# 72 of 80 TensorE transposes done as 32x32 blocks on VectorE, with the blocks moved through a DRAM scratch

## The chip, the cores and the metric

The kernel runs on one core of a Trainium2 chip. A core has TensorE (PE in the profile: matmuls, with the weight loads as PEld), VectorE (DVE), ScalarE (ACT), GpSimd (POOL) and SyncE (SP), each with its own instruction queue worked off in order. Transfers are issued from the queues of SP, ACT or POOL. The metric is the device time of one execution in microseconds; of several runs the median is given.

## What is computed

A decoder trunk of two layers over 256 positions of width 2048, all in 32-bit floats. The even layer runs two token mixers beside each other (HGRN2, a gated linear recurrence done in chunks, and RG-LRU, a per-channel recurrence) on one input projection; the odd layer is an mLSTM. Each branch has a gate path. After the output projection and the residual sum comes a gated per-layer embedding. Cut to what the change touches:

```python
h = x
for i in range(2):
    hn = rmsnorm(h, norm[i])
    u = hn @ w_in[i]
    ...                                            # the mixers of the layer
    y = head_rmsnorm(mixed, g) * gate(u)           # g: a_norm (even, HGRN2 half), c_norm (odd)
    h = h + y @ w_out[i]
    pl = rmsnorm(p[i] @ ple_w[i], ple_norm[i])
    h = h + sigmoid(h @ ple_gate_w[i]) * pl
return rmsnorm(h, final_norm)
```

## The kernel before

A tile has 128 partitions. An activation lies either feature-major (features on the partitions, 256 positions along the row) or token-major (128 positions on the partitions, features along the row, two halves `hf`). A matmul contracts over partitions, so what goes into a projection must be feature-major.

Every projection is done with three matmuls, since a float is split into a high part and a rest: ScalarE casts the raw weight to `whi` (L129), VectorE subtracts to get `wlo` (L130), and activations are split the same way into `hi` and `lo` of one tile `ahl`. `load_weights` loads two raw tiles of 128x1024 (512 KB each, SP's queue, L124). There are five raw buffers and four each of `whi` and `wlo`, so ScalarE can cast as soon as TensorE has freed a buffer. `block` is one feature-major block of 128 outputs: 16 matmuls of 512 columns (L160) with both halves of the activation, then 16 of 256 columns (L166). `project_tok` is the token-major form, a pair of 128x512 outputs in four quarters `kq` of 24 matmuls (L201 to L203).

The work beside the projections is written as generators. `start(lane, gen)` puts one into a lane, `pump()`, called once in every block and quarter, advances each lane by one step, and `drain` finishes a lane. A scheduler then sets the order of each queue from priorities: the two split instructions of a weight tile are given a priority 400 places ahead.

Transposes stand in two places. `feature_major` (L458 to L476) takes a finished token-major tile `u` of 2 x 512 features, transposes its eight 128x128 squares on TensorE into two PSUM banks `mx` (L469), and then scales each by the norm's gain and splits it (`scaled_split`: L278 on ScalarE, L279 on VectorE) into the `ahl` tiles `y` that the output projection reads. It is started twice in the even layer (by `combine`, in the stretch of the `ez` projection and the gates behind it) and four times in the odd layer (one for each `oz` projection `j`). `turn` (L1084 to L1091) transposes a quarter `hq[q]` of the residual stream from feature-major to token-major (L1089), four times in the last stage; the `gated` function there reads the result from PSUM as its last addend (L1097). All six and four calls take eight transposes each, 80 in all.

The last stage is three `project_tok` of `g1`, then `quarter(0)` and `quarter(1)`, two projections of half the width (L1129 to L1131) that share the last turn; then come the final norm and the stores.

## Time and profile before

| | |
|---|---|
| median of 3 runs | 1069.3 us (1068.81 to 1069.33) |
| span of the profiled execution, first to last instruction | 1067.3 us |
| TensorE busy | 1053.7 us, 99% |
| VectorE busy | 744.7 us, 70% |
| ScalarE busy | 583.4 us, 55% |
| GpSimd busy | 121.8 us, 11% |
| HBM traffic | 199.25 MB read, 2.10 MB written |

The page gives no time for the profiled execution but its span; the median of the runs lies 2.0 us above it. In the views, a line such as "L130 DVE TENSOR_TENSOR wlo<-raw,whi ... x359 | 455.8, 1294 | 229.4" names source line, engine, operation, output and inputs, and the count; then come busy microseconds in all, mean nanoseconds of one, and the idle time of the engine before it. The chain is followed back from the last instruction; a piece gives its start, its length and what ran. Overlapping matmuls each show their full duration, but on the chain only what each adds.

### The profile page before, as it was taken

How to read it: one execution, taken by the hardware profiler on the slowest of the kernel's cores; microseconds unless marked ns; L12 is line 12 of the kernel's file. 1: busy time of each engine (PE TensorE's matmuls, PEld its weight loads, DVE VectorE, ACT ScalarE, POOL GpSimd, SP SyncE). 2: the span in 40 equal slices, each digit the busy share in tenths (PEclk: the TensorE clock that was granted, in tenths of full speed). 3: DMA queues.
4: the chain of work that ended last, by engine and by line, in shares of the span. 5: the costliest groups of instructions: out<-in, count | busy, mean ns of one | idle time of the engine just before them, and what ended most of it. 6: DMA issues, size and time to landing. Idle time of an engine off the chain costs nothing.

```text
span 1067.3 us, 16069 instructions
## 1 busy us (share of the span) xinstructions
PE 1053.7 (99%) x6128; PEld 906.2 (85%) x6128; DVE 744.7 (70%) x1090; ACT 583.4 (55%) x854; POOL 121.8 (11%) x96
## 2 busy tenths in 40 slices
PE   8999999999999999999999999999999999999996
PEld 7888888888888888888888888888888888888886
DVE  6778997997767557777444877765556577755665
ACT  7665545869554445656444666644445465434543
POOL 0044532511000000112000000000000003000111
PEclk9999999999999999999999999999999999999998
DMA  9755554545746555555555544455555765655552
GB/s 354 287 182 188 198 165 152 178 159 195 239 159 207 188 196 190 187 181 193 191 196 174 180 158 157 145 183 192 195 186 201 237 213 170 198 197 177 178 178 80
DMA packets 57102, 202.39 MB, mean 190 GB/s; under 512 B 6337, under 2 KB 7617, under 8 KB 57025
## 3 DMA queue, kind: packets, MB, share of 16 engines
q1 hardware_dynamic: 55440, 196.65, 54.9%
q0 software_dynamic: 1152, 4.19, 1.2%
q8 instruction: 48, 0.79, 0.3%
q10 hardware_dynamic: 432, 0.52, 0.1%
q14 instruction: 30, 0.24, 0.1%
HBM read 199.25 MB, written 2.10 MB: 189 GB/s over the span
## 4 chain that ended last, share of the span: by engine, by line
PE 99%; ACT 0%; DMA 0%; DVE 0%; ACTq 0%; issue 0%
PE mm L160 33%; PE mm L166 17%; PE mm L201 13%; PE mm L203 13%; PE mm L202 13%; PE mm L1131 1%; PE mm L1129 1%; PE mm L1130 1%; PE mx L750 1%; PE nu L967 1%; PE mx L469 0%; PE mm L149 0%; PE mx L588 0%; PE mm L150 0%; PE mm L151 0%; PE mm L1046 0%
## 5 line engine op out<-in xcount | busy, mean ns | idle before, releaser
L130 DVE TENSOR_TENSOR wlo<-raw,whi 128x1024 fp32r<-128x1024 f32 (+1 forms) x363 | 457.2, 1285 | 229.4 <-ACT whi L129 135.1
L129 ACT CAST whi<-raw 128x1024 fp32r<-128x1024 f32 (+1 forms) x363 | 377.5, 1044 | 329.2 <-PE mm L160 155.0
L160 PE MATMUL mm<-ahl,whi 128*128 128x512 f32 x1536 | 367.3, 391 | 0.0
L160 PEld LDWEIGHTS mm<-ahl,whi 128*128 128x128 f32 x1536 | 282.1, 188 | 56.4 <-DVE ahl L279 0.7
L201 PE MATMUL mm<-whi,ahl 128*128 128x512 f32 x608 | 239.1, 393 | 0.0
L203 PE MATMUL mm<-whi,ahl 128*128 128x512 f32 x608 | 236.8, 390 | 0.0
L202 PE MATMUL mm<-wlo,ahl 128*128 128x512 f32 x608 | 236.7, 389 | 0.0
L166 PE MATMUL mm<-ahl,wlo 128*128 128x256 f32 x1536 | 202.1, 284 | 0.0
L166 PEld LDWEIGHTS mm<-ahl,wlo 128*128 128x128 f32 x1536 | 195.5, 191 | 7.1 <-issue 0.4
L203 PEld LDWEIGHTS mm<-whi,ahl 128*128 128x128 f32 x608 | 114.1, 188 | 24.0
L201 PEld LDWEIGHTS mm<-whi,ahl 128*128 128x128 f32 x608 | 114.2, 188 | 23.2
L202 PEld LDWEIGHTS mm<-wlo,ahl 128*128 128x128 f32 x608 | 114.2, 188 | 23.1
L172 ACT COPY sm<-mm 128x256 f32<-128x256 f32 x64 | 23.6, 368 | 42.5 <-PE mm L166 42.5
L1029 POOL DMA_DIRECT2D row<-in_rows_dram x4 | 2.2, 540 | 356.8 <-DVE u L1019 336.7
L274 POOL TENSOR_TENSOR acc<-acc,sq 128x512 f32<-128x512 f32 x6 | 9.8, 1633 | 193.7 <-ACT sq L273 193.7
L173 DVE TENSOR_TENSOR mg<-mm,sm 128x256 f32<-128x256 f32 x64 | 26.5, 415 | 0.1
L856 DVE SCALAR_TENSOR_TENSOR qk<-mg,prm,qk 128x255 f32<-128x255 f32 (+2 forms) x48 | 21.1, 478 | 5.0 <-ACT qk L853 4.7
L1117 POOL TENSOR_TENSOR pl<-pl,row 128x512 f32<-128x512 f32 x6 | 9.2, 1535 | 124.7 <-ACT sq L1101 124.7
L1129 PE MATMUL mm<-whi,ahl 128*128 128x256 f32 x64 | 18.3, 285 | 0.0
L274 POOL TENSOR_TENSOR placc<-placc,sq 128x512 f32<-128x512 f32 x7 | 11.2, 1607 | 60.2 <-ACT sq L273 59.8
L1130 PE MATMUL mm<-wlo,ahl 128*128 128x256 f32 x64 | 18.1, 283 | 0.0
L1131 PE MATMUL mm<-whi,ahl 128*128 128x256 f32 x64 | 18.1, 283 | 0.0
(294 smaller groups left out, 809.8 us busy)
## 6 DMA issues: line engine op xcount, KB each, us to landing
raw<-in_ew_dram SPq DMA_DIRECT2D x64, 512.0 KB, 4.3
raw<-in_g_dram SPq DMA_DIRECT2D x56, 512.0 KB, 3.9
raw<-in_eo_dram SPq DMA_DIRECT2D x32, 512.0 KB, 4.1
raw<-in_ov_dram SPq DMA_DIRECT2D x32, 512.0 KB, 3.7
raw<-in_oqk_dram SPq DMA_DIRECT2D x32, 512.0 KB, 4.3
raw<-in_oog_dram SPq DMA_DIRECT2D x32, 512.0 KB, 3.9
raw<-in_oz_dram SPq DMA_DIRECT2D x32, 512.0 KB, 3.9
raw<-in_oo_dram SPq DMA_DIRECT2D x32, 512.0 KB, 4.0
```

The lines of the kernel that those rows point to most:

```text
L129: last["act"] = s.copy(h, r).ins
L130: last["dve"] = v.tensor_tensor(out=l, in0=r, in1=h.bitcast(F32), op=ALU.subtract).ins
L160: last["pe"] = te.matmul(ps, parts[k // 8][0][:, c:c + P], act[k // 2][2][:, (k % 2) * 512:(k % 2 + 1) * 512], start=(k == 0), stop=False).ins
L166: last["pe"] = te.matmul(ps[:, T:2 * T], parts[k // 8][1][:, c:c + P], act[k // 2][0][:, k % 2], start=False, stop=(k == KT - 1)).ins
L172: s.copy(small, ps[:, T:2 * T])
L173: v.tensor_tensor(out=dst, in0=ps[:, 0:T], in1=small, op=ALU.add)
L201: te.matmul(ps[hf], xh, wh, start=(k == 0), stop=False)
L202: te.matmul(ps[hf], xh, wl, start=False, stop=False)
L203: last["pe"] = te.matmul(ps[hf], xl, wh, start=False, stop=(k == KT - 1)).ins
L1129: te.matmul(ps[hf], xh, wh, start=(k == 0), stop=False)
L1130: te.matmul(ps[hf], xh, wl, start=False, stop=False)
L1131: last["pe"] = te.matmul(ps[hf], xl, wh, start=False, stop=(k == KT - 1)).ins
```

## The change

`feature_major` and `turn` no longer use TensorE. VectorE's `transpose` turns each 32x32 block where it lies, written to a tile `w` in an order that groups the blocks by their target. A new function `across` writes `w` to a DRAM scratch tile of its own (512 KB) and reads it back with four transfers into `r`, each filling 32 partitions from runs of 1 KB, so that each block gets to its place. All five transfers are issued from ScalarE's queue. In `feature_major` ScalarE then scales from `r` into `xr` and splits that (`split_act`, L144 and L145); in `turn` it copies `r` to a tile `x`, which `gated` reads in place of the PSUM bank. The last of the four calls in the odd layer (j = 3) keeps the old function, under the name `feature_major_pe`; its eight transposes stay on TensorE. The tiles come from buffers of other tiles: in the even layer from the tags `q` and `f`, in the odd layer from a tag `wt` of four 128x1024 buffers, in which `wt` and `scw` of the mixer now lie too. The last turn is started ahead of the third `g1` projection instead of behind it, in the same lane.

```diff
+    def across(w, r, name):
+
+        d = dr.tile([P, 1024], F32, name=name)
+        s.dma_start(out=d, in_=w)
+        yield
+        to = r.rearrange("p (i n) -> p i n", i=4)
+        for j in range(4):
+            s.dma_start(out=to[32 * j:32 * j + 32], in_=d.rearrange("(i q) (j n) -> j q i n", i=4, j=4)[j])
+        yield
+
+    def feature_major(u, gain, first, y, room):
+
+        w = room("w")
+        w5 = w.rearrange("p (j c h t) -> p h c j t", j=4, c=4, h=2)
+        for hf in range(2):
+            v.transpose(w5[:, hf], u[:, hf].rearrange("p (c j q) -> p c j q", c=4, j=4))
+        yield
+        r = room("r")
+        yield from across(w, r, f"du{gain}{first}")
+        r5 = r.rearrange("p (i c h t) -> p c h i t", i=4, c=4, h=2)
+        for b in range(2):
+            x = tp.tile([P, 512], F32, name="xr", tag="hn", bufs=3)
+            for k in range(2):
+                s.activation(x[:, k * T:(k + 1) * T].rearrange("p (h i t) -> p h i t", h=2, i=4), r5[:, 2 * b + k],
+                             AF.Copy, scale=pc(gain, first + 2 * b + k))
+            y[first // 2 + b] = split_act(x, "y")
+
-    def feature_major(u, gain, first, y):
+    def feature_major_pe(u, gain, first, y):
...
-            start("fm", feature_major(u, "cn", 4 * j, y))
+            start("fm", feature_major(u, "cn", 4 * j, y, room) if j < 3 else feature_major_pe(u, "cn", 4 * j, y))
...
         def turn(q, banks):
 
+            w = room("w")
+            w5 = w.rearrange("p (j h c x) -> p h c j x", j=4, h=2, c=4)
             for hf in range(2):
-                ps = px.tile([P, 512], F32, name="mx", tag="mx")
-                for i in range(4):
-                    te.transpose(ps[:, i * P:(i + 1) * P], hq[q][:, i * T + hf * P:i * T + (hf + 1) * P], ident)
-                banks.append(ps)
-                yield
+                v.transpose(w5[:, hf], hq[q].rearrange("p (c h j t) -> p h c j t", c=4, h=2, j=4)[:, hf])
+            yield
+            r = room("r")
+            yield from across(w, r, f"dh{q}")
+            r5 = r.rearrange("p (i h c x) -> p h c i x", i=4, h=2, c=4)
+            x = room("x")
+            for hf in range(2):
+                s.copy(x[:, hf * 512:(hf + 1) * 512].rearrange("p (c i x) -> p c i x", c=4, i=4), r5[:, hf])
+                banks.append(x[:, hf * 512:(hf + 1) * 512])
...
+        banks = [[] for _ in range(4)]
         for g in range(3):
-            banks = []
-            start("tr", turn(g, banks))
+            start("tr", turn(g, banks[g]))
+            if g == 2:
+                start("tr", turn(3, banks[3]))
             ps = project_tok(a["g1"], g, act)
-            drain("tr")
+            while not banks[g]:
+                step("tr")
```

More of the change, by code (lines that the diff above doesn't have):

```diff
@@ L55, in trunk @@
     pst = ctx.enter_context(tc.tile_pool(name="pst", bufs=2, space=PSUM))
+    dr = ctx.enter_context(tc.tile_pool(name="dr", bufs=1, space=bass.MemoryType.DRAM))
     lanes = {}
@@ L802, in trunk, with room @@
         held = {}
+        def room(which):
+            if which == "w":
+                return m0.tile([P, 1536], F32, name="wu", tag="q")[:, 0:1024]
+            return m0.tile([P, 1024], F32, name="ru", tag="f")
         def combine():
@@ L808, in combine @@
                     v.tensor_tensor(out=u[:, hf], in0=u[:, hf], in1=res["o", g][:, hf], op=ALU.mult)
-                start("fm", feature_major(u, "an", 4 * g, y))
+                start("fm", feature_major(u, "an", 4 * g, y, room))
         for g in range(2):
@@ L878, in trunk, with room @@
         sy.dma_start(out=gr, in_=a["ogf"])
-        wt = m1.tile([P, KT, 32], F32, name="wt", tag="wt", bufs=1)
+        def room(which):
+            return m1.tile([P, 1024], F32, name=which, tag="wt", bufs=4)
+        wt = room("wt")[:, 0:512].rearrange("p (k x) -> p k x", k=KT)
         gp.memset(wt, 0.0)
@@ L940, in mix @@
             p3 = ps.rearrange("p (i t) -> p i t", i=2)
-            wt = m1.tile([P, 2, 384], F32, name="wt", tag="wt", bufs=1)
+            wt = room("wt")[:, 0:768].rearrange("p (i t) -> p i t", i=2)
             v.tensor_tensor(out=wt[:, :, 0:T], in0=tri2.unsqueeze(1).to_broadcast([P, 2, T]), in1=p3, op=ALU.subtract)
@@ L950, in mix @@
             yield
-            scw = m1.tile([P, 2, 384], F32, name="scw", tag="scw", bufs=2)
+            scw = room("scw")[:, 0:768].rearrange("p (i t) -> p i t", i=2)
             for i in range(2):
@@ L1108, in trunk @@
         warm = tp.tile([P, 1], F32, name="warm", tag="warm", bufs=1)
+        banks = [[] for _ in range(4)]
         for g in range(3):
-            banks = []
-            start("tr", turn(g, banks))
+            start("tr", turn(g, banks[g]))
+            if g == 2:
+                start("tr", turn(3, banks[3]))
             ps = project_tok(a["g1"], g, act)
-            drain("tr")
+            while not banks[g]:
+                step("tr")
             for hf in range(2):
                 pl = pls[g][hf]
-                gated(g, ps[hf], banks[hf], pl, hf)
+                gated(g, ps[hf], banks[g][hf], pl, hf)
                 gp.tensor_tensor(out=pl, in0=pl, in1=fnr[g // 2][:, (g % 2) * 512:(g % 2 + 1) * 512], op=ALU.mult)
@@ L1135, in quarter @@
                     yield ps
-        banks = []
-        start("tr", turn(3, banks))
         for ps in quarter(0, [(hf, kq) for kq in range(4) for hf in range(2)]):
@@ L1143, in trunk @@
             pl = pls[3][hf][:, 0:T]
-            gated(3, ps[hf], banks[hf][:, 0:T], pl, hf)
+            gated(3, ps[hf], banks[3][hf][:, 0:T], pl, hf)
             gp.tensor_tensor(out=pl, in0=pl, in1=fnr[1][:, 512:512 + T], op=ALU.mult)
@@ L1150, in trunk @@
             pl = pls[3][hf][:, T:2 * T]
-            gated(4, ps[hf], banks[hf][:, T:2 * T], pl, hf, hf == 0)
+            gated(4, ps[hf], banks[3][hf][:, T:2 * T], pl, hf, hf == 0)
             x = hss[:, 4, hf:hf + 1]
```

## The prediction

> **What bounds the kernel now.** I read the page first: the span, the busy shares and the chain of work that ended last.

> ```profile
> span 1067.3 us, 16069 instructions
> ...
> PE 1053.7 (99%) x6128; PEld 906.2 (85%) x6128; DVE 744.7 (70%) x1090; ACT 583.4 (55%) x854; POOL 121.8 (11%) x96
> ...
> PE 99%; ACT 0%; DMA 0%; DVE 0%; ACTq 0%; issue 0%
> ```

> TensorE is busy throughout and the chain lies on it. A busy PE need not run at its pace, so I then read who waits for whom.

> ```profile
> PE mm L149 <- ACT whi L129: 5.0, 1, 5.0
> ...
> ACT whi L129 <- PE mm L160: 155.0, 113, 2.7
> ...
> ACT whi L129 <- PE mm L203: 130.6, 108, 3.5
> ```

> The first line is the only wait that the view of waits has for PE: 5.0 us at the start. The other two say that ScalarE, which casts the weights into `whi`, waits for TensorE to free a buffer over 220 times. So the feeders run as far ahead as four buffers allow, and TensorE's instruction stream is the time. An instruction taken out of it shortens the span by its place in the stream, as long as the feeders keep their lead.

> How large that place is, the lines of the transposes and the chain tell together:

> ```profile
> L469 PE MATMUL mx<-cst,u x48: 270/272/273, 256.3 to 877.0; 128*128 128x128 f32 x48
> L1089 PE MATMUL mx<-cst,hq x32: 270/272/273, 969.1 to 1038.2; 128*128 128x128 f32 x32
> ...
> 256.22 0.23 PE mm L203
> 256.45 0.87 PE mx L469 x8
> 257.32 0.23 PE mm L201
> ...
> 975.22 0.44 PE mx L1089 x4
> ```

> One transpose lasts 272 ns, but eight together hold the stream for 0.87 us and four for 0.44: 0.109 and 0.110 us each, because they overlap. The 0.110 is what counts.

> **Part 1: 72 transposes leave TensorE.** Of the 48 on L469 the five moved calls issue 40, of the 32 on L1089 all go: 40 x 0.109 + 32 x 0.110 = 4.35 + 3.52 = 7.9 us off the path. The bound above is the whole duration, 72 x 0.272 = 19.6 us; the bound below is nothing, if something else fills the gap. I take 7.9, since the chain has exactly these pieces. Their weight loads go with them. In the built program the rest of TensorE's order is unchanged, but for a few matmuls of `out_proj` by one or five places and for Part 5.

> [...]

> **Part 2: VectorE and ScalarE.** VectorE gets 18 block transposes (nine places, two of 128x512 each). The trace has none; the nearest rows are 128x512 operations from SBUF to SBUF:

> ```profile
> L145 DVE TENSOR_TENSOR ahl<-hq,ahl 128x512 fp32r<-128x512 f32 x16 | 10.7, 690 | 9.6 <-ACT ahl L144 9.6
> L278 ACT ACTIVATE ahl<-mx,prm 128x256 fp32r<-128x256 f32 x24 | 10.8, 472 | 8.4 <-PE mx L469 6.3 <-DVE ahl L279 1.9
> L279 DVE SCALAR_TENSOR_TENSOR ahl<-mx,prm,ahl 128x256 fp32r<-128x256 f32 x24 | 11.1, 480 | 6.6 <-ACT ahl L278 6.4
> L144 ACT CAST ahl<-hq 128x512 fp32r<-128x512 f32 x16 | 9.5, 617 | 6.6 <-DVE hq L365 6.6
> L130 DVE TENSOR_TENSOR wlo<-raw,whi 128x1024 fp32r<-128x1024 f32 x359 | 455.8, 1294 | 229.4 <-ACT whi L129 135.1 <-PE mm L166 59.6 <-issue 18.0
> ```

> I take 0.69 us, between 0.48 and 1.29: 1.4 us a place, 12 us in all. In each of the five `feature_major` calls, four L279 (1.92 us) become two splits of 0.69, so VectorE saves 0.5 there; ScalarE keeps four activations and gains two casts, 1.2 us. Each of the four turns adds two copies on ScalarE, 1.2 us. Beside that every place issues five DMAs from ScalarE's queue. What hides all this is the slack of the stages:

> ```profile
> 243.00:265.00 22.00, 22.00 (x107) 18.49 (x106) 16.77 (x29) 21.85 (x46) 3.99 (x3) 1.00 0.55 180
> 265.00:311.00 46.00, 46.00 (x269) 40.68 (x268) 34.09 (x44) 25.63 (x35) 1.06 (x2) 1.00 0.65 219
> 777.00:865.00 88.00, 88.00 (x402) 73.13 (x401) 54.90 (x65) 42.59 (x51) 2.16 (x4) 1.00 0.63 209
> 966.00:1034.00 68.00, 68.00 (x315) 56.33 (x314) 40.89 (x41) 30.39 (x40) 6.04 (x4) 1.00 0.55 180
> ```

> The columns are the stretch, its length, then busy time of PE, weight load, VectorE, ScalarE and GpSimd, the granted clock (1.00 everywhere), the DMA share and GB/s. In 777 to 865 and 966 to 1034, where six of the nine places lie, VectorE works 62% and 60%, ScalarE 48% and 45% of the time; some 3 us more per 22 us fit. Only 243 to 265 is full for ScalarE (21.85 of 22); there it gains one DMA issue, and its four L278 (1.9 us) move behind 265. I cost Part 2 at nothing.

> **Part 3: five DMAs a place, and their waits on ScalarE's queue.** One write of 512 KB to the scratch, then four reads of 128 KB; the first read waits for the write, the first consumer for the reads, and casts of `whi` stand behind both.

> ```profile
> q1 hardware_dynamic: 55440, 196.65, 54.9%
> ...
> hq<-in_xT_dram POOLq DMA_DIRECT2D x4, 512.0 KB, 5.6
> ...
> xt<-in_x_dram SPq DMA_DIRECT2D x4, 512.0 KB, 10.0
> ...
> out_dram<-pl SPq DMA_DIRECT2D x5, 256.0 KB, 2.9
> ...
> out_dram<-pl SPq DMA_DIRECT2D x4, 128.0 KB, 2.0
> ...
> raw<-in_pw_dram ACTq DMA_DIRECT2D x2, 128.0 KB, 3.7
> ...
> L1179 ACTq DMA_DIRECT2D out_dram<-pl x1: 381/381/381, 1062.1 to 1062.1; - x1
> ```

> An issue from ScalarE takes 0.38 us: 45 x 0.38 = 17 us spread over nine places. A write of 512 KB isn't in the trace: I take 4 us, between the 2.9 of a 256 KB store and the 10.0 of loads in the crowded start; a read 2.0 to 3.7. Moved bytes rise by 9 x 1 MB on 202, on a queue busy 55%. Is the wait covered? Casts come in pairs:

> ```profile
> 1027.98 1.05 ACT L129 CAST whi<-raw 128x1024 fp32r<-128x1024 f32 x1 [2.98 <-PE mm L203]
> 1029.34 1.06 ACT L129 CAST whi<-raw 128x1024 fp32r<-128x1024 f32 x1 [0.31 <-PE mm L203]
> ...
> 1033.42 1.06 ACT L129 CAST whi<-raw 128x1024 fp32r<-128x1024 f32 x1 [0.76 <-PE mm L203]
> ...
> 1034.58 0.28 PE L1129 MATMUL mm<-whi,ahl 128*128 128x256 f32 x1
> ```

> The cast that ends at 1029.03 is first used at 1034.58, 5.55 us later; its `wlo` (1.0 us behind it) has 4.5 us of lead. In the built order the write typically stands behind the first cast of a pair and the first read behind the second. The next pair is not due until 1033.42, 4.4 us after the write. So a landing within 4.4 us costs nothing, and TensorE feels it only beyond 4.4 + 4.5 = 8.9 us. I cost the waits at nothing; without that cover each microsecond beyond 8.9 would cost up to nine. The reads stand between later casts, a quarter of a projection (24 matmuls of 0.227, 5.4 us) before their consumer, so they have more room than they need. Weight loads on SP's queue share completion counters with the new DMAs in turn, but five raw buffers keep them some 8 us ahead of their cast by the same pairs (an estimate: one and a half pairs of 5.4); GpSimd's queue gets nothing new.

> **Part 4: the tail.** The last turn's copy of `hq` is read by the last gate. In the built order its fourth read stands behind the last `whi` cast.

> ```profile
> 1044.33 1.05 ACT L129 CAST whi<-raw 128x1024 fp32r<-128x1024 f32 x1 [1.83 <-PE mm L1131]
> ...
> 1054.92 0.21 DVE L1162 TENSOR_SCALAR fy<-hss 128x1 f32<-128x1 f32 x1 [0.64 <-ACT sq L1101]
> ...
> 1058.68 0.38 ACT L1095 ACTIVATE th<-mm 128x256 f32<-128x256 f32 x1 [0.20 <-PE mm L1131]
> ```

> From 1034.58 to 1058.68 TensorE has 192 quarter matmuls and eight transposes (0.88 us): 0.121 us each. The last cast waits for half of them: 11.6 us after the quarter's start, done at 12.6. The read goes out at 13.0 and lands at 15.0 to 16.7; two copies of 0.6 end at 16.3 to 17.9. Gate arithmetic, two sums of squares and the total need some 3.1 us more, so `fy` starts at 19.4 to 21. Now it starts 3.8 us before the last matmul's consumer, which will be at 23.3: 19.5. So the tail is level or up to 1.5 us later; landings in this stretch meet little other traffic, so I take +0.2.

> **Part 5: the eight transposes that stay** move, in the built order, from behind the embedding projection into it (groups of 2, 3, 3, at about 2.7, 4.3 and 6.0 us after its start), and wait there for `u`.

> ```profile
> 865.35 0.39 PE L1044 MATMUL mm<-whi,ahl 128*128 128x512 f32 x1
> ...
> 869.02 0.48 DVE L1019 SCALAR_TENSOR_TENSOR u<-u,fac,num 128x256 f32<-128x256 f32 x1
> 870.55 0.48 DVE L1019 SCALAR_TENSOR_TENSOR u<-u,fac,num 128x256 f32<-128x256 f32 x1
> ```

> The two late pieces end 4.2 and 5.7 us after the projection's start: TensorE waits 0 to 0.5 us, I take 0.2.

> **Sum.** 1067.3 - 7.9 + 0.2 + 0.2 = 1059.8 us of span. The median of the runs shown, 1069.3, lies 2.0 above this execution's span; with the same 2.0: 1061.8.

> **Rivals.** *Half given back* (faster, by less): somewhere the feeders lose their lead, at 243 to 265 where ScalarE is full, or the tail's reads land late. For it: 21.85 of 22. Against it: the four L278 that leave. Price: 1.5 us in the tail in place of 0.2, and 0.7 us at three places: +3.4, 1065.2.

> *The round trip is exposed* (slower): at the first read ScalarE waits for the write, the casts behind it come late, TensorE waits. For it: 10.0 us landings exist in this trace. Against it: they are from its first microseconds, and hq's 5.6 is the worst later. At 10.0 each of nine places loses 1.1: +9.9, 1071.7. It turns slower than before from about 9.7 us a landing (0.83 x 9 = 7.5). [...]

> *No change*: VectorE or ScalarE sets the pace where the lead is gone, and takes back what TensorE frees: 1067.2 to 1071.4. For it: VectorE at 70%. Against it: the 220 waits of ScalarE for TensorE.

> **How the numbers follow.** Forecast 0.68, half given back 0.14, no change 0.07, slower 0.11. This kernel's measurement tells 0.2%, 2.1 us, from no change; so faster 0.82, same 0.07, slower 0.11. The likeliest case alone spans 1060.5 to 1063.0: 1061.8 with 1.3 less (no wait anywhere, and the whole effect of switching between kinds of matmul) or 1.2 more. The range reaches into the second case: 1060.3 to 1067.0.

> **What would show it.** Right: PE still 99% of the chain, no L469 or L1089 group but eight transposes, PE's only long wait still the one at the start, first reads waiting on ScalarE within 4.4 us of slack. Wrong: PE waiting for `whi` or `wlo`, writes landing after 8.9 us, block transposes far over 1.29 us, or a last matmul more than 10 us before the end.

## The result, and the profile after

The changed kernel takes 1076.3 us (median of 4 runs, 1074.4 to 1079.2) where the kernel before takes 1069.2 on the same chip: a ratio of 1.0069, 95% interval 1.0053 to 1.0084. It is 7.1 us slower. The forecast was 1061.8, faster by 7.5.

The page of the changed kernel and its view of waits (what PE waited for: us in total, times, longest):

```profile
span 1072.6 us, 16023 instructions
...
PE 1049.1 (98%) x6056; PEld 900.9 (84%) x6056; DVE 751.8 (70%) x1098; ACT 591.4 (55%) x872; POOL 120.0 (11%) x96
...
PE 96%; DMA 2%; ACT 1%; DVE 1%; issue 0%; ACTq 0%
```

```profile
PE mm L161 <- DVE mg L174: 5.3, 1, 5.3
PE mm L150 <- ACT whi L130: 5.0, 1, 5.0
PE mm L1081 <- DVE u L512: 4.2, 1, 4.2
```

The busy shares have hardly moved: VectorE 70% as before, ScalarE 55%. What is new is two waits of TensorE and 2% of the chain on DMA. The 5.0 us at the start was there before. The other two are both waits for a PSUM bank: TensorE starts a new group of matmuls into the pool `pm`, which has three banks, and the old content of the bank has not been read yet by VectorE (`mg`, the merge of a gate block, at 281: ScalarE copies one half of the bank to `sm`, VectorE adds the other half to it; and `u`, the gate of the last `oz` projection, at 870).

**The odd layer, around 870.** The time line of the three engines (start, length, engine, line, what; in brackets the idle time before it and what ended it):

```profile
862.25 0.31 ACTq L466 DMA_DIRECT2D r<-ducn  x1
...
871.40 0.51 ACT L482 ACTIVATE xr<-r,prm 128x256 f32<-128x256 f32 x1 [4.02 <-DMA r<-ducn]
871.82 1.03 ACT L130 CAST whi<-raw 128x1024 fp32r<-128x1024 f32 x1
...
872.88 1.23 DVE L131 TENSOR_TENSOR wlo<-raw,whi 128x1024 fp32r<-128x1024 f32 x1 [3.84 <-ACT whi L130]
874.02 0.68 DVE L512 SCALAR_TENSOR_TENSOR u<-u,mm 128x512 f32<-128x512 f32 x1
...
874.75 0.80 PE L1081 MATMUL mm<-whi,ahl 128*128 128x512 f32 x1 [4.17 <-DVE u L512]
```

Read it upwards. TensorE waits for `u` on VectorE; `u` stands behind a weight split `wlo`; that waits for a cast `whi`; the cast stands on ScalarE behind `xr`; and `xr` has waited 4.02 us for the last of the four reads, which went out at 862.25 and was there at 871.2: 9.0 us. The activation that `u` needs from ScalarE stands behind `xr` as well, at 872.75. No engine was short of time here; four things stood in a row in two queues.

**The even layer, around 281**, ScalarE and then VectorE:

```profile
273.45 0.31 ACTq L466 DMA_DIRECT2D ru<-duan  x1
274.40 0.37 ACT L173 COPY sm<-mm 128x256 f32<-128x256 f32 x1
275.36 0.37 ACT L173 COPY sm<-mm 128x256 f32<-128x256 f32 x1 [0.59 <-PE mm L167]
...
281.13 0.91 ACT L482 ACTIVATE xr<-ru,prm 128x256 f32<-128x256 f32 x2 [2.88 <-DMA ru<-duan]
```

```profile
283.01 1.23 DVE L131 TENSOR_TENSOR wlo<-raw,whi 128x1024 fp32r<-128x1024 f32 x1 [1.76 <-ACT whi L130]
284.15 0.68 DVE L146 TENSOR_TENSOR ahl<-xr,ahl 128x512 fp32r<-128x512 f32 x1
284.99 0.69 DVE L146 TENSOR_TENSOR ahl<-xr,ahl 128x512 fp32r<-128x512 f32 x1 [0.15 <-ACT ahl L145]
285.60 0.75 DVE L174 TENSOR_TENSOR mg<-mm,sm 128x256 f32<-128x256 f32 x2
```

The merges need the copies `sm`, done at 274.8 and 275.7. But in VectorE's queue they stand behind weight splits, the last of which waits for a cast that stands behind `xr`, and behind the two splits of the transposed tile (L146), which cannot run before ScalarE has the reads. So they run at 285.60, ten microseconds late, and hold two of the three banks. In the kernel before, such a merge had only a pair of weight splits ahead of it and ran about 1 us behind its copy, which was done at 277.0:

```profile
278.02 0.42 DVE L173 TENSOR_TENSOR mg<-mm,sm 128x256 f32<-128x256 f32 x1
```

**Why the reads are late.** One suspect is the loads that GpSimd issues. The last two of its loads of `hq`, before and then after:

```profile
271.93 0.53 POOL L828 DMA_DIRECT2D hq<-in_xT_dram  x1 [13.76 <-DVE u L808]
281.43 0.53 POOL L828 DMA_DIRECT2D hq<-in_xT_dram  x1 [8.97 <-PE mx L469]
```

```profile
270.68 0.53 POOL L861 DMA_DIRECT2D hq<-in_xT_dram  x1 [18.40 <-DVE u L841]
273.90 0.53 POOL L861 DMA_DIRECT2D hq<-in_xT_dram  x1 [2.70 <-DVE wu L474]
```

These loads of 512 KB wait for buffers that `u` leaves. The transposes on TensorE let go of `u` late (`PE mx`), those on VectorE at once (`DVE wu`): the last load goes out 7.5 us earlier, 0.5 us behind the read. The four norm rows of the odd layer go out in pairs in the same way, at 829.9 and 831.8, 850.7 and 851.9, where they stood some 11 us apart before. The stretches around both waits, before and then after (the last two columns are the share of the DMA engines and GB/s, ahead of them the granted clock):

```profile
272.00:284.00 12.00, 12.00 (x73) 10.66 (x72) 8.55 (x12) 6.48 (x9) 0.99 (x2) 1.00 0.79 259
...
854.00:870.00 16.00, 16.00 (x76) 13.34 (x75) 12.39 (x17) 10.01 (x14) 0.53 (x1) 1.00 0.66 215
```

```profile
272.00:284.00 12.00, 8.88 (x55) 7.80 (x53) 6.19 (x7) 6.30 (x11) 0.53 (x1) 1.00 0.95 335
854.00:870.00 16.00, 16.00 (x73) 13.23 (x72) 8.16 (x9) 5.96 (x6) 0.00 (x0) 1.00 0.98 303
```

The DMA engines go from 0.79 and 0.66 to 0.95 and 0.98; the scratch transfers of the change itself are in that too, so what the loads do is left to an experiment. With those engines full, a 128 KB read on ScalarE's queue takes up to 10.3 us, where the least in the execution is 2.5 and the median 4.9.

**The price of a wait is more than its length.** The stretches behind the first wait:

```profile
284.00:286.00 2.00, 0.00 (x0) 0.00 (x0) 1.85 (x5) 0.92 (x2) 0.00 (x0) 0.91 0.58 86
286.00:288.00 2.00, 1.84 (x4) 1.49 (x5) 1.37 (x4) 0.81 (x2) 0.00 (x0) 0.50 0.87 330
```

The granted clock is down to 0.50 when the matmuls start again. From the starts of successive matmuls, against the median of the same pair of lines, the two waits are 5.4 and 4.4 us, and in the 9 us behind each another 1.5 and 2.5 us go: 13.8 us together. Take 13.8 from the span of 1072.6 and 1058.8 are left, 1 us below the forecast's 1059.8. This is the account of the profiled execution, which at 1074.4 us is the fastest of the four; the others had a lower mean granted clock (0.990 to 0.992 against 0.993), and their waits are not on record.

### The profile page after: what moved, and what is told of

It is laid out like the page before. It is cut to its first block, busy times and chain, and to the rows that moved or that the text cites. A ratio compares the mean times of both kernels' runs of the same rounds, so it can differ in the third digit from the quotient of the medians.

```text
span 1072.6 us, 16023 instructions
## 1 busy us (share of the span) xinstructions
PE 1049.1 (98%) x6056; PEld 900.9 (84%) x6056; DVE 751.8 (70%) x1098; ACT 591.4 (55%) x872; POOL 120.0 (11%) x96
## 3 DMA queue, kind: packets, MB, share of 16 engines
q1 hardware_dynamic: 55440, 196.65, 54.8%
## 4 chain that ended last, share of the span: by engine, by line
PE 96%; DMA 2%; ACT 1%; DVE 1%; issue 0%; ACTq 0%
PE mm L161 33%; PE mm L167 17%; PE mm L202 13%; PE mm L203 13%; PE mm L204 13%; DMA r<-ducn 1%; DMA ru<-duan 1%; PE mx L778 1%; PE nu L1004 1%; PE mm L1177 1%; PE mm L1176 1%; PE mm L1175 1%; PE mx L616 0%; PE mm L150 0%; PE mm L152 0%; PE mm L151 0%
## 5 line engine op out<-in xcount | busy, mean ns | idle before, releaser
L130 ACT CAST whi<-raw 128x1024 fp32r<-128x1024 f32 (+1 forms) x363 | 377.2, 1043 | 338.1 <-PE mm L161 155.7
L203 PE MATMUL mm<-wlo,ahl 128*128 128x512 f32 x608 | 236.6, 389 | 0.0
L203 PEld LDWEIGHTS mm<-wlo,ahl 128*128 128x128 f32 x608 | 114.2, 188 | 23.5
L1163 POOL TENSOR_TENSOR pl<-pl,row 128x512 f32<-128x512 f32 x6 | 9.7, 1614 | 121.4 <-ACT sq L1144 121.4
L1108 POOL TENSOR_TENSOR pl<-pl,row 128x512 f32<-128x512 f32 x8 | 13.0, 1646 | 50.9 <-ACT sq L1107 50.9
## 6 DMA issues: line engine op xcount, KB each, us to landing
raw<-in_ew_dram SPq DMA_DIRECT2D x64, 512.0 KB, 4.4
raw<-in_g_dram SPq DMA_DIRECT2D x56, 512.0 KB, 4.0
raw<-in_eo_dram SPq DMA_DIRECT2D x32, 512.0 KB, 4.3
raw<-in_ov_dram SPq DMA_DIRECT2D x32, 512.0 KB, 3.8
raw<-in_oqk_dram SPq DMA_DIRECT2D x32, 512.0 KB, 4.1
raw<-in_oog_dram SPq DMA_DIRECT2D x32, 512.0 KB, 4.0
raw<-in_oz_dram SPq DMA_DIRECT2D x32, 512.0 KB, 4.4
raw<-in_oo_dram SPq DMA_DIRECT2D x32, 512.0 KB, 3.8
```

The lines of the kernel that those rows point to most:

```text
L130: last["act"] = s.copy(h, r).ins
L203: te.matmul(ps[hf], xh, wl, start=False, stop=False)
```

## The experiments

The theory: the loss sits in these two places alone, and there in the order of ScalarE's and VectorE's queues behind late reads. The rivals: the round trip is too slow wherever it stands; GpSimd's loads do it by themselves; the short runs of the reads do it; the transfers slow TensorE by way of the weights. Times are medians, beside 1069 for the kernel before on the same chip.

**The turns alone.**

```diff
-                start("fm", feature_major(u, "an", 4 * g, y, room))
+                start("fm", feature_major_pe(u, "an", 4 * g, y))
...
-            start("fm", feature_major(u, "cn", 4 * j, y, room) if j < 3 else feature_major_pe(u, "cn", 4 * j, y))
+            start("fm", feature_major_pe(u, "cn", 4 * j, y))
```

> Only the four turns keep the VectorE transposes; all six feature_major calls are back on TensorE. Theory (the loss sits at two places, in the even layer at 280 and in the odd at 870, where reads of feature_major land late): the turns cost nothing and 32 transposes x 0.110 = 3.5 us are saved, 1069.2 - 3.5 = 1065.7, between 1065.2 and 1067.2 with the tail up to 1.5 later; TensorE has no wait but the 5.0 us at the start. Rival (a round trip through DRAM is too slow at any place): four of the nine places should bear four ninths of the change's loss, 1072 or more.

Measured: 1065.6 us, ratio 0.9966 (0.9954 to 0.9979). The span fell from 1067.3 to 1063.8, the 3.5 us of 32 transposes, and TensorE waits only at the start. So four of the nine round trips cost nothing, and the place in the stream (0.110 us a transpose) is the right measure of the gain.

**The consumers queued later.**

```diff
         yield from across(w, r, f"du{gain}{first}")
+        for _ in range(4 if gain == "an" else 1):
+            yield
...
+        with tc.issue_after(last["act"]):
...
```

> Every transfer stays where it is; only ScalarE's four activations that read the landed blocks, and the two casts behind them, are queued later (in the even layer by some three weight casts, in the odd layer's third call behind all casts of the embedding projection). Theory (ScalarE stands in order behind a late read, VectorE's freeing of PSUM behind ScalarE): both new waits of TensorE go, 7.9 us are saved but for 0.4, 1061.7, at most 1064. Rival (the transfers themselves slow the weight loads and TensorE waits for those): nothing changes, 1074 to 1078, and the waits of TensorE stay in another form. Reads still land in 2.5 to 10 us in either case.

Measured: 1068.1 us (ratio 0.9993, 0.9984 to 1.0002). That is above the 1064 expected: 8 us came back, of 14. Both old waits are gone, but the edit pushed the even layer's second place too far; the output projection now waits for its splits:

```profile
PE mm L161 <- DVE ahl L146: 3.8, 1, 3.8
```

**GpSimd's loads held back.**

```diff
+        if i >= 2:
+            gp.tensor_copy(t[:, 0:1], y[3][2][:, 0:1].bitcast(F32))
         gp.dma_start(out=t, in_=a["xT"][:, i * 1024:(i + 1) * 1024])
...
+                gp.tensor_copy(t[:, 0:1], y[5][2][:, 0:1].bitcast(F32))
                 gp.dma_start(out=t, in_=a["rows"][i, b * 1024:(b + 1) * 1024].partition_broadcast(P))
```

> The work is that of the changed kernel, but GpSimd's loads of the last two quarters of the residual stream and of the four norm rows wait until the last place's reads have been used, by a one-column copy in front of each. Theory that these loads, which the change lets out earlier and in pairs, make the reads late: the reads at 273 and 862 land in 3 to 5 us in place of 7.6 and 9.0, no wait of ScalarE over 1 us there, and the time falls to 1062 to 1065. Rival (the reads are late by the weight loads or by their runs of 1 KB alone): they still land after 7 us or more and the time stays at 1073 to 1078.

Measured: 1066.2 us (ratio 0.9971, 0.9962 to 0.9981), above the range, so the expectation was half right. The DMA share falls to 0.71 from 272 to 284 and to 0.73 from 854 to 870. The odd layer's read now lands in 3.3 us and `xr`, 5.0 us behind it, waits for nothing; in the even layer the read lands in 5.1 us and ScalarE waits 0.40 us, and yet TensorE waits there, 3.2 us:

```profile
860.78 0.31 ACTq L466 DMA_DIRECT2D r<-ducn  x1
...
865.81 0.51 ACT L482 ACTIVATE xr<-r,prm 128x256 f32<-128x256 f32 x1
```

```profile
274.12 0.31 ACTq L466 DMA_DIRECT2D ru<-duan  x1
...
279.32 0.91 ACT L482 ACTIVATE xr<-ru,prm 128x256 f32<-128x256 f32 x2 [0.40 <-DMA ru<-duan]
```

```profile
282.97 1.28 DVE L146 TENSOR_TENSOR ahl<-xr,ahl 128x512 fp32r<-128x512 f32 x2
284.18 0.75 DVE L174 TENSOR_TENSOR mg<-mm,sm 128x256 f32<-128x256 f32 x2
```

So the crowding is real, and without it the odd layer's wait is gone but for 0.2 us. The even layer's wait does not need a late read: the merges behind the two splits suffice, and the late read only made it longer (5.3 us in place of 3.2).

**Both edits**, the lines of the two experiments above together:

> Both edits together. If either cause alone explains the loss, it is gone here as well: 1061.7 to 1064, TensorE's only wait the 5.0 us at the start. If neither does, above 1069, and TensorE waits for something not yet named; a new wait for the loads that are held (the residual sum of the even output projection, or the norm rows) would show as a wait of VectorE or GpSimd for hq or row.

Measured: 1067.15 us (ratio 0.9982, 0.9973 to 0.9991). This lies between what was expected if one cause alone explained the loss and what if none did. The wait at 310 that the edit of the consumers had made is there again (3.8 us), and no other but the one at the start; it says nothing more than the two before.

**The merges first**, on the changed kernel with nothing else altered (`merge_up[0]` is 400 in the even layer's gate blocks and 0 elsewhere):

```diff
+        with tc.high_priority(offset=merge_up[0]):
             s.copy(small, ps[:, T:2 * T])
             v.tensor_tensor(out=dst, in0=ps[:, 0:T], in1=small, op=ALU.add)
...
```

> The changed kernel, with the merges of the even layer's gate blocks given a priority 400 places ahead, so that VectorE's queue has them ahead of one weight split and of the two splits of the transposed tile; transfers and ScalarE's order around them stay. Theory (in the even layer it is VectorE's order, not the read alone: the copies that the merges need were done at 274.8 and 275.7, but the merges, which free PSUM, stood behind the splits until 285.6): the wait at 280 goes, the one at 870 stays; of the 7 us that the even layer loses (5.4 of wait and 1.6 of lower clock) some 6 to 7 come back, 1069 to 1070.5. Rival (the late read stops the weight casts and with them TensorE, whatever VectorE's order): TensorE waits for a cast or a weight split there instead, 2 us or more, and the time stays at 1073 to 1078.

Measured: 1067.6 us (ratio 0.9987, 0.9978 to 0.9997), 8.7 us faster than the changed kernel, more than expected. ScalarE now stands still for 5.68 us, about twice as long as in the changed kernel, and the consumer starts 8.6 us after the read went out (the bracket names a weight load, but the read itself lands 8.5 us after its issue, just ahead of the consumer). TensorE waits 0.8 us there all the same, and 3.0 us in the odd layer, which this edit leaves alone:

```profile
275.67 0.31 ACTq L469 DMA_DIRECT2D ru<-duan  x1
...
284.24 0.51 ACT L485 ACTIVATE xr<-ru,prm 128x256 f32<-128x256 f32 x1 [5.68 <-DMA raw<-in_ew_dram]
```

```profile
PE mm L1086 <- DVE u L515: 3.0, 1, 3.0
PE mm L161 <- DVE mg L177: 0.8, 1, 0.8
```

That settles the even layer: with the read even later than in the changed kernel (8.5 us against 7.6), 4.5 of the 5.3 us of wait are gone. What made it was what VectorE had queued behind the late read.

**The first consumer later, in a lane of its own.** As in the second experiment, but for the even layer's first place and the odd layer's third alone, and with a lane for each place of the even layer:

```diff
         yield from across(w, r, f"du{gain}{first}")
+        n = (4 if first == 0 else 0) if gain == "an" else int(first == 8)
+        for _ in range(n):
+            yield
...
+        with ExitStack() as order:
+            if n:
+                order.enter_context(tc.issue_after(last["act"]))
...
-                start("fm", feature_major(u, "an", 4 * g, y, room))
+                start(f"fm{g}", feature_major(u, "an", 4 * g, y, room))
```

> The edit of the queued-later kernel, without its mistake: the consumer of the even layer's first place moves behind some four more weight casts, the second place has a lane of its own and stays where the changed kernel has it, the odd layer's third consumer stands behind the embedding projection's casts. GpSimd's loads are not held. Theory (order decides, crowding alone does not): no new wait of TensorE, 1061.7, range 1061 to 1063.5. Rival (without holding the loads the transfers come too late anyway): one wait of 2 us or more in the even layer, 1065 to 1068.

Measured: 1064.4 us (ratio 0.9955, 0.9938 to 0.9972), 4.6 us faster than the kernel before, but above the range of the theory. The waits at 281 and 870 are gone. A wait of 2.7 us at 292 has come, for a merge again. ScalarE stands at the first reads of the even layer's second place until its write, issued at 274.4, has landed 11.6 us later; its next cast starts only at 287.06 (the bracket names a weight load, but the reads stand ahead of it). And the copies for two merges stand behind three casts more:

```profile
287.06 1.05 ACT L130 CAST whi<-raw 128x1024 fp32r<-128x1024 f32 x1 [5.34 <-DMA raw<-in_ew_dram]
...
292.39 0.64 ACT L173 COPY sm<-mm 128x256 f32<-128x256 f32 x2
```

Which of the two it is, the late write or the place of the copies, the next run tells.

**The same with the loads held**, by the lines of the third experiment:

> The same with GpSimd's loads held as before. Theory: the loads cost nothing more once the order gives slack, the same time as without holding, 1061.7 within 1. Rival (crowding costs by itself): 1 to 4 us faster than the kernel that only queues the consumer later.

Measured: 1064.4 us (ratio 0.9957, 0.9943 to 0.9972), the same to 0.1 us, but not the 1061.7 of the theory: the wait at 292 is there too (2.6 us). Here the write lands in at most 7.3 us and ScalarE does not stand behind it for 5 us, and yet the two copies run together and late, behind the casts:

```profile
289.91 1.05 ACT L130 CAST whi<-raw 128x1024 fp32r<-128x1024 f32 x1 [0.76 <-PE mm L161]
...
291.38 0.64 ACT L173 COPY sm<-mm 128x256 f32<-128x256 f32 x2
```

The first of the two had its matmuls done at 286.2. So the late write is not needed for this wait; that the copies stand behind weight casts, and the merges behind weight splits, is enough: an order that this edit left. And once the consumers stand later, holding the loads brings nothing more.

**Runs of 4 KB.**

```diff
-            s.dma_start(out=to[32 * j:32 * j + 32], in_=d.rearrange("(i q) (j n) -> j q i n", i=4, j=4)[j])
+            s.dma_start(out=to[32 * j:32 * j + 32], in_=d[32 * j:32 * j + 32].rearrange("q (i n) -> q i n", i=4))
```

> The changed kernel, but the four reads of a place take 32 rows as they were written, in runs of 4 KB in place of 1 KB: the blocks are not moved to their place, so the kernel leaves that part of the transposes out; issues, bytes and waits are the same. Rival (the reads land late because of their short runs): reads of the third odd place land in 3 to 5 us in place of 9, the wait at 870 goes, 1068 to 1071. Theory (the reads are late because they share the engines with weights and GpSimd's loads, and the order does the rest): landings shorten by 1 to 2 us at most, one or both waits stay, 1072 to 1077.

Measured: 1072.8 us (ratio 1.0033, 1.0020 to 1.0046). Landings shorten from a median of 4.9 us (longest 10.3) to 4.1 (8.8), the last read of the third odd place lands in 6.9 us and not in 3 to 5, and both waits stay, at 4.1 and 2.1 us. The short runs have a part of 3.5 us in the loss; they are not what makes it.

**Both edits of order.** The merges first, and the consumers of the first even and the third odd place queued later, with a lane for each place of the even layer as above; against the kernel with the first consumer later, only the lines of the merges are new:

```diff
+        n = (4 if first == 0 else 0) if gain == "an" else int(first == 8)
...
+            merge_up[0] = 400
             y[4 + j] = gate_mul(j)
+            merge_up[0] = 0
...
```

> Both edits of order on the changed kernel, GpSimd's loads not held: the even layer's merges first in VectorE's queue, the consumers of the even layer's first place and of the odd layer's third queued later. Transfers, their bytes and the work are those of the changed kernel. Theory (only the order behind late reads was wrong): TensorE has no wait over 1 us but the one at the start; the kernel that only queued the consumer later lost 2.7 us at 292 and some 1 us of lower clock there, so 1064.4 - 3 to 3.7 = 1060.7 to 1061.7, the time that the prediction had. Rival (the transfers cost something everywhere, by slower weights or by VectorE's port): 1063 to 1066 with no wait to be seen, matmuls spaced wider.

Measured: 1061.9 us (1060.9 to 1062.3), ratio 0.9932 (0.9920 to 0.9945): 7.0 us faster than the kernel before on the same chip, where the forecast for the change had 7.5. Its span and its waits:

```profile
span 1059.3 us, 16022 instructions
```

```profile
PE mm L150 <- ACT whi L130: 5.0, 1, 5.0
PE mm L152 <- DVE wlo L131: 0.3, 1, 0.3
```

The transfers are as late as ever, and the DMA engines as full (0.97 from 272 to 284, and 0.97 from 847 to 863, where this kernel, some 7 us ahead by then, does what the changed one does from 854 to 870):

```profile
855.37 0.31 ACTq L469 DMA_DIRECT2D r<-ducn  x1
...
861.77 0.68 ACT L520 ACTIVATE u<-mm,rth 128x512 f32<-128x512 f32 x1
...
864.27 0.91 ACT L491 ACTIVATE xr<-r,prm 128x256 f32<-128x256 f32 x2 [1.35 <-DMA r<-ducn]
```

The read takes 8.7 us, as against 9.0, and ScalarE waits 1.35 us for it. But the activation `u`, which VectorE needs before it can free the gate's bank, now stands ahead of that wait. In the even layer ScalarE even stands 5.5 us behind the second place's write, which lands in 9.2, and TensorE has no wait. Between 1076 and 1062 lies order alone: the same transfers are as late in both. Nor are the matmuls spaced wider, as the rival had it: on the chain the 16 of 512 columns in a block take 3.65 us and the 16 of 256 columns 1.91, as in the kernel before. A port of VectorE was a guess, which no run shows.

**The merges first, and only the odd layer's third consumer later**, against the kernel with both edits of order:

```diff
-        n = (4 if first == 0 else 0) if gain == "an" else int(first == 8)
+        n = (0 if first == 0 else 0) if gain == "an" else int(first == 8)
```

> The merges first, and of the consumers only that of the odd layer's third place queued later. Theory: the kernel with the merges first lost 0.8 us at 281 and 3.0 at 865 with their clock (in all 5.1 over its even spacing); the second goes, the first stays: 1067.6 less 3.1 to 4.5 = 1063 to 1064.5. Rival (moving the odd consumer only moves the wait): a new wait of TensorE in the embedding projection or at the start of the output projection, 1066 or more.

Measured: 1063.0 us (ratio 0.9946, 0.9933 to 0.9960), in the range. The wait of 0.8 us in the even layer stays, as expected; in the odd layer 1.2 us are left, at a copy out of PSUM in the embedding projection, which is the rival's mechanism at a smaller size. With the even layer's first consumer later as well, the time is 1.1 us less.

**A control: the merges first in the kernel before**, with the same three lines:

> The kernel before with the same priority for the merges of the even layer's gate blocks, as a control: TensorE has no wait there, so nothing is to be had, 1069.2 within 0.5. Were it faster by 2 us or more, the gain of the merges would not be evidence on the change.

Measured: 1069.3 us (ratio 1.0005, 0.9996 to 1.0014), no change: the priority gains only where the change has put something ahead of the merges.

**A wait by itself.** In the kernel before, two weight casts of one `oog` projection are each done seven times over:

```diff
-                    last["act"] = s.copy(h, r).ins
+                    for _ in range(7 if src is delayed.get("w") else 1):
+                        last["act"] = s.copy(h, r).ins
...
```

> The kernel before, with one pair of weight casts of the third oog projection done seven times over (12 casts more, 11.4 us of ScalarE), so that TensorE runs dry once, in a place that the change doesn't touch and with no transfer added. Measured by itself: what a wait of TensorE costs beside its own length. Theory (after a wait of some microseconds the granted clock is about half for a few us, as behind both waits of the changed kernel): a wait w of 2 to 7 us, and the span grows by w + 1.5 to 3 us. Rival (the lower clock there came from the transfers): the granted clock stays at 1.00 behind the wait, and the span grows by w alone, within 0.5.

Measured: 1076.6 us (ratio 1.0069, 1.0052 to 1.0086), 7.4 us slower for a wait of 4.9, so 2.5 us beside its length, as the theory had it:

```profile
PE mm L207 <- ACT whi L132: 4.9, 1, 4.9
```

```profile
738.00:742.00 4.00, 0.00 (x0) 0.00 (x0) 0.00 (x0) 4.00 (x5) 0.00 (x0) 0.85 0.00 0
742.00:744.00 2.00, 1.29 (x3) 0.57 (x3) 1.23 (x1) 2.00 (x3) 0.00 (x0) 0.50 0.00 0
744.00:746.00 2.00, 2.00 (x5) 1.61 (x6) 0.51 (x1) 2.00 (x3) 0.00 (x0) 0.50 0.53 121
```

For the first 6 us there is no transfer at all in this stretch, and the clock still goes to 0.50 for 4 us and more. So the low clock comes with the wait and needs no transfer.

## Why the prediction was wrong

**The bound was right.** TensorE's stream is the time, and what leaves it is won: 3.5 us for 32 transposes alone, and 7.0 us at the median for all 72 once nothing waits (1068.9 to 1061.9; Parts 1, 4 and 5 had 7.5 together). The two profiled executions differ by 8.0 us of span (1067.3 to 1059.3), but the second is among the fastest of its five. That this kernel's 1061.9 agrees to 0.1 us with the 1061.8 of the forecast is in part luck, since its chip was 0.4 us faster for the kernel before too.

**Part 1 was right**: 0.110 us a transpose, not the 0.272 of its duration, as the turns alone show.

**Part 2 was right in its sizes**: the block transposes take 0.70 us (0.69 forecast). Its "nothing" was read from busy shares, and these say nothing of what stands behind what: in the even layer the new splits stand ahead of the merges, and there VectorE's part was not free.

```profile
L474 DVE STREAM_TRANSPOSE w<-u 128x512 f32<-128x512 f32 x6 | 4.1, 704 | 0.1
```

**Part 3 failed**, in the sentence "I cost the waits at nothing". In its place the profiled execution lost 9.8 us of TensorE's time to two waits and 4.0 to the clock behind them. It failed at four points:

- *Sizes.* A read was put at 2.0 to 3.7 us, from 128 KB transfers elsewhere in the execution; the two that mattered took 7.6 and 9.0. The same view of the kernel before has a 128 KB load of 5.2 us, which the range left out, and the 5.6 us of `hq`, called the worst, is a median; the slowest took 7.4. The reads were said to have a quarter of a projection, 5.4 us, "more room than they need". That room was right (ScalarE came to the consumer 5.1 us after the odd read's issue) and was too small. The write was put at 4 us and took 5.0 at the median, 8.1 at the most.
- *The lead that was counted.* The limit of 8.9 us was the lead of the weight casts. It was the wrong chain: the lead that ran out first, at both places, was that of a PSUM bank, three in the pool, freed by VectorE's merges and gates. The prediction never asked what in VectorE's queue stands behind the new splits. In the even layer this made a wait of 3.2 us with a read as quick as 5.1 us; with the merges first, a consumer 8.6 us behind its read cost TensorE 0.8 us.
- *The other queue.* "GpSimd's queue gets nothing new" was true of its instructions and wrong of its times: a tile that is let go earlier lets the load that waits for its buffer go earlier, into the same microseconds as the reads. With these loads held, the odd layer's read landed in 3.3 us. The completion counters that the prediction names are in the trace of the changed kernel: ScalarE's 48 transfers, 45 of them new, signal on the same eight semaphores as SP's 385, and GpSimd's eight on others; what that costs was not tried.
- *The price.* A wait was priced at its length. Each of these two cost 1.5 and 2.5 us more by the clock behind it.

**Part 4 was right.** In the last stage TensorE has no new wait; `fy` of the first half starts 3.5 us ahead of the last matmul's consumer, against 3.8 before, and ScalarE's last instruction starts 4.3 us behind the last matmul's start, against 4.1: the 0.2 of the forecast. **Part 5 was cheaper than said.** With the loads held, where no long wait of TensorE stands ahead of them, the eight transposes that stay ran in their three groups without waiting for `u`; in the kernel with both edits of order they all run behind the embedding projection, so there the term is not tested.

**The rivals.** The one that ended slower had the right mechanism in part, ScalarE standing before a round trip that is late, but at the wrong place: it priced nine places by the casts, and it turned at 9.7 us a landing. What happened is two places, by the banks, and in the even layer with a landing of 5.1 us already. No rival had VectorE's order in it. The signs listed for being wrong did not come in their form either: TensorE waited for `mg` and `u`, not for `whi` or `wlo`, and no write took longer than 8.1 us.

## What to carry to other kernels

Before a new wait is costed at nothing, list what stands behind the waiting instruction on its own queue, and then what stands behind *that* on the next engine's queue, down to whatever frees a PSUM bank: the shortest lead on this chain is the slack, and here it was shorter than the lead of the weights. When a resource is let go earlier, look for the transfer that is waiting for it. If a round trip is late at one or two places, try the order first (consumers behind, what frees banks ahead): here that turned 1.0069 into 0.9932 with the same transfers.

## What the runs showed of the hardware

**The clock behind a wait.** By the starts of the matmuls, in the 9 us behind a wait of TensorE: waits of 5.4, 5.05, 4.4, 4.3 and 4.0 us lost another 1.5, 2.4, 2.5, 2.7 and 2.6 us; waits of 3.3 and 3.2 us lost 1.4 and 1.9; waits of 1.0 and 1.4 us lost at most 0.4. In between it went both ways, in two kernels that differ little but in the held loads: 2.9 us with the first consumer later, and then 2.7 us in the same with the loads held:

```profile
296.00:298.00 2.00, 2.00 (x10) 1.66 (x9) 1.87 (x4) 1.32 (x2) 0.00 (x0) 1.00 0.76 248
```

```profile
296.00:298.00 2.00, 2.00 (x6) 1.58 (x5) 1.32 (x2) 0.88 (x1) 0.00 (x0) 0.50 0.42 158
```

**Landings.** The same 128 KB read took 2.5 us at the least and 10.3 at the most within one execution, the slowest at 859, where GpSimd's loads, the weights and the scratch fill the DMA engines to 0.98. Whether more queues or other issuing engines would shorten them was not tried.
